# First weights loaded ahead of the constants, low parts of w_out made on VectorE, U blocks redistributed over the routing and gate-matrix stages, gate loads written as three separate thirds

## The chip, the cores and the metric

The kernel runs on one core of a Trainium2 chip. The metric is the device time of one execution in microseconds; smaller is better. Times given as "span" are from the first to the last instruction of one profiled execution.

## What is computed

One decoder block on x of 512 tokens by 1024 channels, all in fp32:

```python
h  = rmsnorm(x) ; z = h @ w_in + b_in              # 1024 x 5376
conv_out = silu(layernorm(conv31(val * sigmoid(gate)))) @ w_conv_out
attn_out = sliding_window_attention(rope(q), rope(k), v, sinks) @ w_attn_o
x  = x + (sigmoid(g_conv)*conv_out + sigmoid(g_attn)*attn_out) @ w_out
h2 = rmsnorm(x)
q  = h2 @ w_pq ; for 8 heads: top 16 of 128 + 128 sub-key scores -> 16 of 16384 experts, softmax gate
x  = x + sum over the chosen experts of gate * gelu(u_emb[e] . h2) * v_emb[e]
out = rmsnorm(x)
```

The tokens form four chunks of 128. For chunk 0 the experts' rows are gathered one by one. For the three other chunks ("dense") the products with all 16384 experts are computed as matrix products: a gate matrix G (experts by tokens, mostly zero) is built, U blocks give gelu(u_emb . h2) for 128 experts at a time, and V steps add (G * gelu) times 128 rows of v_emb.

## The kernel before, in words

Every weight is split into a high part that TensorE multiplies fast and a low rest. `load_w` (L120) does it for one block of 128 x 1024: SP issues the load into `wraw` (L122, three buffers), ScalarE (ACT) rounds it into `whi` (L124, four buffers), and `wlo` is made in one of two ways. With `by_dma` off, VectorE (DVE) subtracts (L130). With it on, ACT writes minus the high part (L127) and a second transfer, issued by GpSimd (POOL, L128), adds the weights from memory to it. `products` (L133) then runs 8 x (high weight by high and by low activation) and 8 x (low weight by high activation): lines L138, L139, L142.

The stages in order of time are:

- Start: SP issues x, g1, ident (L209 to L212), `pc` (L213) and six small constants (L221 to L226); only then come the first weights. Each chunk is normalized and transposed (L183 to L185); the first two blocks of w_in (a gate and a value block) are multiplied in two half-widths by `halves` (L150), and `by_dma` is switched on behind them (L297).
- w_in blocks, rotary tables, the 31-tap convolution on DVE (L283, L286) and the attention, interleaved.
- w_ao and w_co blocks (L441 to L450), then w_out (L458 to L482): two passes of eight weight blocks, each with 12 products of 512 columns (L466, L467, L471), the second pass's halves behind them; after each pass x2 = x + result (L477), the norm, and transposes into tT.
- Routing: for each of eight heads two w_pq blocks, the scores, and the top-16 search on DVE (L495 to L570), each followed by `up(U_HEAD)`, four U blocks (`u_step`, L659).
- Gate matrix: `build_g` (L587), three chunks of eight groups of 16 tokens. DVE makes the one-hot factors (L608, L611), PE multiplies them (L616), ACT copies them out (L618), and SP writes a group to memory (L619). Eight U blocks are handed out over the 24 groups (L708 to L717), so that `AHEAD` = 40 U blocks are done before the last stage.
- Last stage (L728): for i in 0 to 127 one U block (while there are any left) and one V step (18 products, L687 to L689). V steps read the gates of eight steps from one tile `gl` of two buffers, loaded by three transfers (one for each dense chunk, L671) at i % 8 = `GL_AT` = 4 for the next eight steps; DVE multiplies them by the U results (L676), ACT and DVE split them (L680, L681). Beside that POOL gathers the 256 rows of chunk 0 (L624; DVE L639 and L647), paced so that they end at the share `R_V` = 0.99 of the stage's work.

The order of the instructions on each engine isn't the order of the code: a scheduler with a simulated timeline places them, one queue for each engine, and every engine works through its queue in order.

Of the kernel before, what the change touches and what calls it, by code (L numbers as in the profile page):

```python
# [9 lines left out]
F32 = mybir.dt.float32  # L10
# [7 lines left out]
P = 128  # L18
# [9 lines left out]
HEADS = 8  # L28
# [6 lines left out]
DENSE = tuple(b for b in range(NB) if b not in ROW_CHUNKS)  # L35
BUILT = DENSE
ND = len(DENSE)
NU = ND * P
CAND = 80

AHEAD = 40
U_HEAD = 4
ROWS = 4
GT = 16
GI = 8
R_G = 0.0
R_V = 0.99
UC = 3
N_TAPS = 7
XT = 4  # L50
# [2 lines left out]
LOW = 16  # L53
WARM = 0
WARM2 = 0
GL_AT = 4
WRAW = 3
WHL = 4
GLU1 = 4
# [2 lines left out]
J_VAL, J_GATE, J_Q, J_K, J_V, J_GC, J_GA = 0, 8, 16, 24, 25, 26, 34  # L62
# [16 lines left out]
def body(ctx: ExitStack, tc: tile.TileContext, a, out):  # L79
# [10 lines left out]
    def psum(tag):  # L90
        return ps.tile([P, S], F32, name=tag, tag=tag, bufs=2)
# [21 lines left out]
    def load_g(name):  # L113
        g = keep.tile([P, D], F32, name="g")
        nc.sync.dma_start(g, a[name].to_broadcast([P, D]))
        return g

    by_dma = [False]

    def load_w(src):  # L120
        raw = wp.tile([P, D], F32, name="wraw", bufs=WRAW)
        nc.sync.dma_start(raw, src)  # L122
        hi = wp.tile([P, D], F32R, name="whi", bufs=WHL)
        nc.scalar.activation(hi, raw, AF.Copy)  # L124
        lo = wp.tile([P, D], F32R, name="wlo", bufs=WHL)
        if by_dma[0]:
            nc.scalar.activation(lo, hi.bitcast(F32), AF.Copy, scale=-1.0)  # L127
            nc.gpsimd.dma_start(lo, src, accum_op=OP.add)  # L128
        else:
            nc.vector.tensor_tensor(lo, raw, hi.bitcast(F32), op=OP.subtract)  # L130
        return hi, lo
# [39 lines left out]
    def rmsnorm(dst, src, g):  # L171
        ss = small.tile([P, 1], F32, name="n_ss")
        nc.scalar.activation(dst, src, AF.Square, accum_out=ss)
        r = rstd_of(ss, D, [small.tile([P, 1], F32, name=f"n_{x}") for x in "vtr"])
        nc.vector.scalar_tensor_tensor(dst, src, r, g, op0=OP.mult, op1=OP.mult)

    def transpose_split(dst, cs, src):
        hi, lo = dst
        for q in range(2):
            ks = slice(4 * q, 4 * q + 4)  # L180
            p = psum("tr").rearrange("p (a b) -> p a b", a=4)
            for i in range(4):
                nc.tensor.transpose(p[:, i], src[:, (4 * q + i) * P:(4 * q + i + 1) * P], ident)  # L183
            nc.scalar.activation(hi[:, ks, cs], p, AF.Copy)  # L184
            nc.vector.tensor_tensor(lo[:, ks, cs], p, hi[:, ks, cs].bitcast(F32), op=OP.subtract)  # L185

    def chunk(b):
        return slice(b * P, (b + 1) * P)

    def pair_x(name):  # L190
        return [keep.tile([P, KB, S], F32R, name=name + x, tag="x" + x) for x in "hl"]
# [16 lines left out]
    for b in range(NB):  # L208
        nc.sync.dma_start(xs[:, b], a["x"][chunk(b), :])  # L209
        if b == 0:  # L210
            g1 = load_g("g1")
            nc.sync.dma_start(ident, a["ident"])  # L212
    nc.sync.dma_start(pc, a["pc"])  # L213
    h1 = fr.tile([P, NB, D], F32, name="h1", tag="sgc")
    hT = pair_x("hT")
# [239 lines left out]
    h2 = fr.tile([P, NB, D], F32, name="h2", tag="sgc")  # L455
    g2 = load_g("g2")
    tT = pair_x("tT")
    for b0 in range(0, NB, 2):  # L458
        acc = [psum(t) for t in (("ot", "ot", "sc", "sc") if b0 == 0 else ("sc", "sc", "mm", "mm"))]
        for k in range(KB):  # L460
            hi, lo = load_w(a["w_out"][k])
            for c in range(2):
                for n in range(2):
                    ns = slice(n * 512, (n + 1) * 512)
                    p, cs = acc[2 * c + n], chunk(b0 + c)
                    nc.tensor.matmul(p, mT[0][:, k, cs], hi[:, ns], start=(k == 0), stop=False)  # L466
                    nc.tensor.matmul(p, mT[1][:, k, cs], hi[:, ns], start=False, stop=False)  # L467
            for c in range(2):
                for n in range(2):
                    ns = slice(n * 512, (n + 1) * 512)  # L470
                    nc.tensor.matmul(acc[2 * c + n], mT[0][:, k, chunk(b0 + c)], lo[:, ns], start=False,  # L471
                                     stop=(k == KB - 1))
        for c in range(2):
            b = b0 + c
            for n in range(2):
                ns = slice(n * 512, (n + 1) * 512)
                nc.vector.tensor_tensor(x2[:, b, ns], x2[:, b, ns], acc[2 * c + n], op=OP.add)  # L477
            nc.sync.dma_start(x2d[b], x2[:, b])
            rmsnorm(h2[:, b], x2[:, b], g2)
            if b in h2d:  # L480
                nc.sync.dma_start(h2d[b], h2[:, b])
            transpose_split(tT, chunk(b), h2[:, b])  # L482
    fctx.close()

    rp = ctx.enter_context(tc.tile_pool(name="rp", bufs=1, reuse_waits="tile"))
    eidx = rp.tile([P, len(ROW_CHUNKS), SLOTS], U32, name="eidx")
# [170 lines left out]
    gl = {}  # L657

    def u_step(i):  # L659
        w = load_w(a["put"][i])  # L660
        p = psum("mm")[:, :NU]
        products(p, w, [t[:, :, S - NU:] for t in tT])
        g = tp.tile([P, NU], F32, name="ga", bufs=AHEAD + 1)
        nc.scalar.activation(g, p, AF.Gelu)
        ga[i] = g

    def load_gates(i):
        if i < P:
            gl[i // GI] = vp.tile([P, NU // GT, GI, GT], F32, name="gl", bufs=2)
            for n, b in enumerate(DENSE):  # L670
                nc.sync.dma_start(gl[i // GI][:, n * NG:(n + 1) * NG], gv[b][:, :, i:i + GI, :])  # L671

    def v_operands(i):
# [25 lines left out]
    def up(n):  # L699
        for _ in range(n):  # L700
            i = next(ups, None)
            if i is not None:
                u_step(i)

    for h in range(HEADS):
        head(h)
        up(U_HEAD)
    left, groups = AHEAD - HEADS * U_HEAD, len(BUILT) * (P // GT)  # L708
    done = 0
    for b in BUILT:  # L710
        keys(b)
        for _ in build_g(b):
            done += 1
            while done * (AHEAD - HEADS * U_HEAD) > (AHEAD - HEADS * U_HEAD - left) * groups:
                up(1)
                left -= 1
    up(left)  # L717
    by_dma[0] = False
    gctx.close()
    vp = ctx.enter_context(tc.tile_pool(name="vp", bufs=1, reuse_waits="tile"))  # L720
# [3 lines left out]
    rowgen = by_rows()  # L724
    total, due = 2.0 * P - AHEAD, 0.0
    load_gates(0)
    last = {}
    for i in range(P):  # L728
        up(1)
        if i % GI == GL_AT:  # L730
            load_gates(i - GL_AT + GI)
        if i < P - 2:
            v_steps(i)
        elif i == P - 2:
            for _ in rowgen:
                pass
            for n, b in enumerate(DENSE):
                last[n] = rows.tile([P, D], F32, name="row", bufs=ROWS)
                nc.sync.dma_start(last[n], x2d[b])
            v_steps(i, i + 1)  # L740
        due += (2 if i + AHEAD < P else 1) * 2 * SLOTS * len(ROW_CHUNKS) / (R_V * total)
        while due >= 1:
            due -= 1
            next(rowgen, None)
# [59 lines left out]
```

## Time and profile before

| | |
|---|---|
| median of 3 runs | 1836.05 us (1832.74 to 1837.63) |
| the profiled execution's own time | 1836.21 us |
| its span | 1834.4 us, so 1.8 us lie around it |
| PE busy | 1734.7 us (95%) |
| PE weight loads (PEld) | 1519.7 us (83%) |
| DVE busy | 1346.5 us (73%) |
| ACT busy | 918.5 us (50%) |
| POOL busy | 463.9 us (25%) |
| chain that ended last | PE 85%, DMA 5%, DVE 5%, issue 3%, ACT 1% |

PE is TensorE's products, PEld its weight loads. A line such as "L130 DVE" is an instruction group of line 130 on VectorE. The chain that ended last goes back from the last instruction to what released each step. PE is busy for 95% of the span, so the question for a change is in which stretches PE waits or runs at its lower clock, and whose work ends there.

### The profile page before, as it was taken

The page shows a single profiled execution, that of the slowest core. Times are in us where ns is not written, and L with a number is a line of the kernel's source. Part 1 is how long each engine was busy: PE and PEld are TensorE (multiplying, and loading weights), DVE is VectorE, ACT ScalarE, POOL GpSimd, SP SyncE. Part 2 cuts the span into 40 slices and gives each one's busy share as a digit, 9 for nine tenths or more (in the row PEclk, how much of TensorE's full clock was granted, in tenths as well). Part 3 has the DMA queues.
Part 4 walks back from the last instruction along what each step waited for, and adds up shares of the span by engine and source line. Part 5 has one row for each costly group of instructions (what it writes and reads, how often), then busy time and mean ns, then how long its engine had stood idle before and what let it go on. Part 6 is the DMA issues. An engine that isn't in the chain of part 4 may idle for free.

```text
span 1834.4 us, 25060 instructions
## 1 busy us (share of the span) xinstructions
PE 1734.7 (95%) x8892; PEld 1519.7 (83%) x8892; DVE 1346.5 (73%) x2741; ACT 918.5 (50%) x1297; POOL 463.9 (25%) x388
## 2 busy tenths in 40 slices
PE   6999999998899999977599999999999999999996
PEld 6887767786799999966489999999999999988774
DVE  7899992731478787688687768768768767778775
ACT  6449987646565666566533333333333333333332
POOL 1111100112111111000034344424325424434430
PEclk9999998999999999999899999999999999999998
DMA  8996554799999999643678898888889879888884
GB/s 240 230 219 137 132 115 105 172 251 273 254 228 214 225 217 228 199 178 167 229 270 304 271 331 305 294 301 302 308 275 335 304 276 330 309 288 314 302 289 137
DMA packets 167725, 452.21 MB, mean 247 GB/s; under 512 B 14768, under 2 KB 66480, under 8 KB 164528
## 3 DMA queue, kind: packets, MB, share of 16 engines
q0 software_dynamic: 55296, 201.35, 41.8%
q1 hardware_dynamic: 112304, 249.26, 37.9%
q8 instruction: 70, 1.15, 0.2%
q14 instruction: 55, 0.45, 0.1%
HBM read 417.78 MB, written 29.88 MB: 244 GB/s over the span
## 4 chain that ended last, share of the span: by engine, by line
PE 85%; DMA 5%; DVE 5%; issue 3%; ACT 1%; SPq 0%; POOL 0%; DVEq 0%; POOLq 0%; ACTq 0%
PE mm L138 17%; PE mm L139 17%; PE mm L142 17%; PE sc L616 4%; PE tr L689 3%; PE tr L687 3%; PE tr L688 3%; PE sc L688 3%; PE sc L687 3%; PE sc L689 3%; PE ot L687 3%; PE ot L689 3%; PE ot L688 3%; DMA gl<-gb 2%; DMA wlo<-w_out 1%
## 5 line engine op out<-in xcount | busy, mean ns | idle before, releaser
L124 ACT ACTIVATE whi<-wraw 128x1024 fp32r<-128x1024 f32 x346 | 364.9, 1056 | 374.0 <-PE mm L139 200.1
L139 PE MATMUL mm<-tTl,whi 128*128 128x384 f32 (+2 forms) x1168 | 397.5, 341 | 0.2 <-DVE tTl L185 0.2
L138 PE MATMUL mm<-tTh,whi 128*128 128x384 f32 (+2 forms) x1168 | 396.1, 340 | 1.5 <-DVE x L477 1.4
L130 DVE TENSOR_TENSOR wlo<-wraw,whi 128x1024 fp32r<-128x1024 f32 x218 | 265.9, 1221 | 44.3 <-ACT whi L124 40.1
L624 POOL DMA_INDIRECT row<-pu,eidx x128 | 173.0, 1352 | 433.7 <-DVE row L639 270.0
L624 POOL DMA_INDIRECT row<-pv,eidx x128 | 179.8, 1405 | 271.0 <-DVE acc L647 246.6
L680 ACT ACTIVATE wh<-gl 128x384 fp32r<-128x384 f32 x128 | 67.2, 525 | 350.0 <-PE ot L688 321.3
L142 PE MATMUL mm<-tTh,wlo 128*128 128x384 f32 (+2 forms) x1168 | 235.0, 340 | 0.0
L138 PEld LDWEIGHTS mm<-tTh,whi 128*128 128x128 f32 x1168 | 220.3, 189 | 10.0 <-ACT wlo L127 1.8
L139 PEld LDWEIGHTS mm<-tTl,whi 128*128 128x128 f32 x1168 | 220.3, 189 | 8.4 <-DVE tTl L185 0.4
L142 PEld LDWEIGHTS mm<-tTh,wlo 128*128 128x128 f32 x1168 | 204.3, 188 | 3.8
L286 DVE SCALAR_TENSOR_TENSOR yconv<-uc,pc,yconv 128x512 f32<-128x512 f32 x240 | 168.5, 744 | 0.5
L647 DVE SCALAR_TENSOR_TENSOR acc<-row,gate,acc 128x1024 f32<-128x1024 f32 x128 | 163.9, 1280 | 3.6 <-DMA row<-pv,eidx 2.9
L639 DVE SCALAR_TENSOR_TENSOR row<-row,hrow 128x1024 f32<-128x1024 f32 x128 | 155.0, 1220 | 13.7 <-DMA row<-pu,eidx 13.6
L127 ACT ACTIVATE wlo<-whi 128x1024 fp32r<-128x1024 f32 x128 | 134.9, 1055 | 16.6 <-PE mm L142 12.2
L138 PE MATMUL mm<-hTh,whi 128*128 128x512 f32 (+1 forms) x352 | 137.0, 392 | 3.5 <-ACT hTh L184 2.6
L616 PE MATMUL sc<-xt,yt 128*128 128x128 f32 x768 | 110.3, 296 | 31.1 <-DVE xt L611 28.4
L139 PE MATMUL mm<-hTl,whi 128*128 128x512 f32 (+1 forms) x352 | 135.9, 389 | 0.0
L616 PEld LDWEIGHTS sc<-xt,yt 128*128 128x128 f32 x768 | 99.6, 205 | 41.6 <-issue 22.1
L681 DVE TENSOR_TENSOR wl<-gl,wh 128x384 fp32r<-128x384 f32 x128 | 71.1, 556 | 83.1 <-ACT wh L680 78.4
L676 DVE TENSOR_TENSOR gl<-gl,ga 128x384 f32<-128x384 f32 x128 | 61.8, 553 | 90.7 <-DMA gl<-gb 90.7
L618 ACT ACTIVATE gst<-sc 128x512 f32<-128x512 f32 x96 | 99.3, 1064 | 53.5 <-PE sc L616 45.8
(252 smaller groups left out, 3126.3 us busy)
## 6 DMA issues: line engine op xcount, KB each, us to landing
wraw<-put SPq DMA_DIRECT2D x128, 512.0 KB
wraw<-pv SPq DMA_DIRECT2D x128, 512.0 KB
gb<-gst SPq DMA_DIRECT2D x24, 1024.0 KB
gl<-gb SPq DMA_DIRECT2D x48, 512.0 KB
wraw<-w_in SPq DMA_DIRECT2D x42, 512.0 KB
wlo<-w_in POOLq DMA_DIRECT2D x40, 512.0 KB
wlo<-put POOLq DMA_DIRECT2D x40, 512.0 KB
wraw<-w_out SPq DMA_DIRECT2D x16, 512.0 KB
```

The costliest lines, as they stand in the source:

```text
L124: nc.scalar.activation(hi, raw, AF.Copy)
L130: nc.vector.tensor_tensor(lo, raw, hi.bitcast(F32), op=OP.subtract)
L138: nc.tensor.matmul(p, wh[:, ks], xh[:, k], start=(k == 0), stop=False)
L139: nc.tensor.matmul(p, wh[:, ks], xl[:, k], start=False, stop=False)
L142: pace[0] = nc.tensor.matmul(p, wl[:, ks], xh[:, k], start=False, stop=(k == KB - 1))
L286: nc.vector.scalar_tensor_tensor(y[:, j], uc[:, t:t + S], w, y[:, j], op0=OP.mult, op1=OP.add)
L616: nc.tensor.matmul(p[:, t], yt[:, t1 + t], xt[:, t1 + t].rearrange("p a b -> p (a b)"), start=True, stop=True)
L624: ins = nc.gpsimd.indirect_dma_start(out=r, out_offset=None, in_=table, in_offset=bass.IndirectOffsetOnAxis(ap=eidx[:, ROW_CHUNKS.index(b) ...
L647: nc.vector.scalar_tensor_tensor(acc, r, gate[:, b, s:s + 1], acc, op0=OP.mult, op1=OP.add)
L687: nc.tensor.matmul(p, w[0][:, chunk(n)], v[0][:, ns], start=(i == 0), stop=False)
L688: nc.tensor.matmul(p, w[0][:, chunk(n)], v[1][:, ns], start=False, stop=False)
L689: pace[0] = nc.tensor.matmul(p, w[1][:, chunk(n)], v[0][:, ns], start=False, stop=(i == P - 1))
```

## The change

1. Two blocks of w_in are fetched right behind the four chunks of x, ahead of `pc` and the small constants; `load_w` takes them from the list `fetched`.
2. `by_dma` is off for the w_out stage, so that its 16 low parts are made by DVE (L130) and not by ACT (L127) and a transfer (L128); it is on again for the routing stage.
3. U blocks: 4 for each of the first four heads and 3 for each of the others (28, 32 before); 11 over the groups of the gate matrix (8 before); 3 behind it (none before). `AHEAD` is 42 (40 before), so two fewer are left for the last stage.
4. The gate loads of eight steps are issued one at each of i % 8 = 2, 3 and 4, instead of three at 4.
5. `R_V` is 0.96 instead of 0.99: the rows of chunk 0 are gathered at a higher rate and end earlier.

```diff
-AHEAD = 40
-U_HEAD = 4
+AHEAD = 42
+U_HEADS = (4, 4, 4, 4, 3, 3, 3, 3)
+U_LAST = 3
-R_V = 0.99
+R_V = 0.96
-GL_AT = 4
+GL_AT = 2
...
+    fetched = []
+    def fetch(src):
         raw = wp.tile([P, D], F32, name="wraw", bufs=WRAW)
         nc.sync.dma_start(raw, src)
+        return raw
+    def load_w(src):
+        raw = fetched.pop(0) if fetched else fetch(src)
...
+    fetched += [fetch(a["w_in"][j]) for j in (J_GATE, J_VAL)]
     nc.sync.dma_start(pc, a["pc"])
...
     tT = pair_x("tT")
+    by_dma[0] = False
     for b0 in range(0, NB, 2):
...
     fctx.close()
+    by_dma[0] = True
...
-    def load_gates(i):
+    def load_gates(i, blocks=range(ND)):
         if i < P:
-            gl[i // GI] = vp.tile([P, NU // GT, GI, GT], F32, name="gl", bufs=2)
-            for n, b in enumerate(DENSE):
+            if 0 in blocks:
+                gl[i // GI] = vp.tile([P, NU // GT, GI, GT], F32, name="gl", bufs=2)
+            for n in blocks:
+                b = DENSE[n]
                 nc.sync.dma_start(gl[i // GI][:, n * NG:(n + 1) * NG], gv[b][:, :, i:i + GI, :])
...
         head(h)
-        up(U_HEAD)
+        up(U_HEADS[h])
+    spread, groups, done = AHEAD - U_LAST - sum(U_HEADS), len(BUILT) * (P // GT), 0
     for b in BUILT:
         keys(b)
         for _ in build_g(b):
+            up((done + 1) * spread // groups - done * spread // groups)
             done += 1
...
-    up(left)
+    up(U_LAST)
     by_dma[0] = False
...
         up(1)
-        if i % GI == GL_AT:
-            load_gates(i - GL_AT + GI)
+        if 0 <= i % GI - GL_AT < ND:
+            load_gates(i - i % GI + GI, (i % GI - GL_AT,))
```

What the scheduler makes of it is seen in the queues. Lines of the changed kernel have other numbers: its L125 is the load of L122, L137 the subtraction of L130, L486 the addition of L477, L626 the gate product of L616, L145, L146 and L149 the products of L138, L139 and L142, L699 and L700 those of L687 and L688, L683 the gate load of L671. A row counts instructions of the program; PE's fp32 products of L616 appear twice each in a trace.

First DVE's queue at w_out. Before, nothing stands between the last split of `m` and the first addition of the result:

```order
L450 TENSOR_TENSOR ml<-sgc,mh 128x512
L477 TENSOR_TENSOR x_3560<-x_3560,ot 128x512 x2
L477 TENSOR_TENSOR x_3560<-x_3560,sc 128x512 x2
L162 TENSOR_SCALAR n_v<-n_ss 128x1 x2
L164 RECIPROCAL n_r<-n_t 128x1
```

and now:

```order
L458 TENSOR_TENSOR ml<-sgc,mh 128x512
L137 TENSOR_TENSOR wlo<-wraw,whi 128x1024 x6
L486 TENSOR_TENSOR x_3560<-x_3560,ot 128x512 x2
L486 TENSOR_TENSOR x_3560<-x_3560,sc 128x512 x2
L137 TENSOR_TENSOR wlo<-wraw,whi 128x1024
L169 TENSOR_SCALAR n_v<-n_ss 128x1 x2
L171 RECIPROCAL n_r<-n_t 128x1 x2
```

Sixteen subtractions have joined the queue: five between the merge's last blocks, six here, one behind the additions and four behind the first pass's norms.

Second PE's queue at the end of the gate matrix (`sc<-xt,yt` are its products, `mm<-tT..` those of U blocks, `tr<-..,wh` the first V step). Before:

```order
L139 MATMUL mm<-tTl,whi 128x384
L142 MATMUL mm<-tTh,wlo 128x384 x8
L616 MATMUL sc<-xt,yt 128x128 x320
L687 MATMUL tr<-whi,wh 128x512
L688 MATMUL tr<-wlo,wh 128x512
```

and now:

```order
L146 MATMUL mm<-tTl,whi 128x384
L149 MATMUL mm<-tTh,wlo 128x384 x8
L626 MATMUL sc<-xt,yt 128x128 x280
L699 MATMUL tr<-whi,wh 128x512
L700 MATMUL tr<-wlo,wh 128x512
```

In both all U blocks stand ahead of the long run of gate products, and a V step right behind it; the run has become shorter by 40 products. Ahead of it U blocks and half groups of 8 gate products alternate, 8 half groups before and 13 now.

Third SP's queue in the last stage, where the gate loads (`gl`) stand among the loads of `pv`. Before:

```order
L122 DMA wraw<-pv 128x1024 x8
L671 DMA gl<-gb_80 128x8x128
L671 DMA gl<-gb_81 128x8x128
L671 DMA gl<-gb_82 128x8x128
L122 DMA wraw<-pv 128x1024 x10
L739 DMA row<-x2d_76 128x1024
L739 DMA row<-x2d_77 128x1024
L739 DMA row<-x2d_78 128x1024
L122 DMA wraw<-pv 128x1024 x2
L654 DMA out<-wraw 128x1024 x4
```

and now:

```order
L125 DMA wraw<-pv 128x1024 x8
L683 DMA gl<-gb_80 128x8x128
L683 DMA gl<-gb_81 128x8x128
L683 DMA gl<-gb_82 128x8x128
L125 DMA wraw<-pv 128x1024 x5
L748 DMA row<-x2d_76 128x1024
L748 DMA row<-x2d_77 128x1024
L748 DMA row<-x2d_78 128x1024
L125 DMA wraw<-pv 128x1024 x2
L664 DMA out<-wraw 128x1024
L125 DMA wraw<-pv 128x1024 x5
L664 DMA out<-wraw 128x1024 x3
```

The three gate loads still stand side by side with 12 loads of `pv` behind them in both; the loads of x2 (`row<-x2d`) and the first store of the output have moved ahead by five.

## Rows read from the trace of the kernel before

**Rows 1.** Windows: stretch, length; busy us (instructions) of PE, PEld, DVE, ACT, POOL; clock, DMA, GB/s
```profile
0.00:34.30 34.30, 20.36 (x137) 18.98 (x137) 21.84 (x74) 21.80 (x35) 2.19 (x6) 1.00 0.81 252
34.30:263.00 228.70, 228.66 (x1146) 180.57 (x1146) 215.52 (x391) 168.10 (x319) 30.19 (x35) 1.00 0.75 175
412.00:474.00 62.00, 52.47 (x209) 39.69 (x207) 11.38 (x26) 39.24 (x44) 13.85 (x16) 0.92 1.02 271
...
501.57:677.89 176.32, 176.32 (x961) 164.80 (x961) 140.92 (x735) 107.68 (x126) 31.10 (x36) 1.00 0.95 221
...
734.50:774.70 40.20, 40.20 (x276) 40.16 (x275) 26.45 (x39) 23.49 (x28) 2.27 (x2) 1.00 0.61 196
774.70:905.00 130.30, 98.28 (x667) 87.58 (x666) 113.64 (x190) 86.23 (x84) 3.52 (x3) 0.93 0.46 186
905.00:918.00 13.00, 0.24 (x1) 0.24 (x2) 1.41 (x3) 0.95 (x4) 0.00 (x0) 0.54 0.79 260
...
1635.00:1803.60 168.60, 161.60 (x692) 132.56 (x691) 133.60 (x151) 54.73 (x75) 70.29 (x47) 0.97 0.82 287
1803.60:1820.20 16.60, 10.78 (x36) 8.32 (x35) 6.75 (x12) 5.05 (x7) 0.00 (x0) 0.79 0.34 127
```

**Rows 2.** Waits of PE: line, awaited; us in total, times, longest
```profile
PE sc L616 <- DVE xt L611: 28.4, 34, 2.2
PE tr L687 <- ACT wh L680: 13.7, 1, 13.7
...
PE tr L689 <- DVE wl L681: 7.0, 2, 4.1
PE tr L687 <- ACT whi L124: 5.8, 1, 5.8
PE mm L471 <- DMA wlo<-w_out: 4.0, 2, 2.4
PE sc L471 <- DMA wlo<-w_out: 3.3, 3, 2.4
...
PE ot L471 <- DMA wlo<-w_out: 2.2, 4, 0.8
```

**Rows 3.** Chain that ended last, whole span: start, length, what
```profile
3.08 7.18 DMA xs<-x
10.28 5.13 DMA wraw<-w_in
...
432.26 12.65 DMA wlo<-w_out
...
501.57 1.39 PE mm L142 x8
505.73 1.39 PE mm L142 x8
...
1665.62 12.08 DMA gl<-gb
```

**Rows 4.** Waits of DVE, 8 to 40 us
```profile
DVE uc L304 <- ACT sg L300: 2.8, 1, 2.8
```

**Rows 5.** Chain that ended last, in the w_out stage
```profile
412.16 0.24 PE ot L466
...
414.95 0.23 PE ot L466
...
447.03 0.43 PE mm L466
...
454.80 0.87 PE tr L183 x8
...
473.10 0.51 PE sc L471
```

**Rows 6.** Costliest groups: the subtraction; busy, mean ns, idle before
```profile
L130 DVE TENSOR_TENSOR wlo<-wraw,whi 128x1024 fp32r<-128x1024 f32 x218 | 265.9, 1221 | 44.3 <-ACT whi L124 40.1
```

**Rows 7.** Waits of DVE, 1635 to 1810 us
```profile
DVE gl L676 <- DMA gl<-gb: 19.2, 3, 9.4
```

More of the change, by code (lines that the diff above doesn't have):

```diff
@@ L118, in body @@
     by_dma = [False]
-    def load_w(src):
+    fetched = []
+    def fetch(src):
         raw = wp.tile([P, D], F32, name="wraw", bufs=WRAW)
         nc.sync.dma_start(raw, src)
+        return raw
+    def load_w(src):
+        raw = fetched.pop(0) if fetched else fetch(src)
         hi = wp.tile([P, D], F32R, name="whi", bufs=WHL)
@@ L706, in body @@
         head(h)
-        up(U_HEAD)
-    left, groups = AHEAD - HEADS * U_HEAD, len(BUILT) * (P // GT)
-    done = 0
+        up(U_HEADS[h])
+    spread, groups, done = AHEAD - U_LAST - sum(U_HEADS), len(BUILT) * (P // GT), 0
     for b in BUILT:
@@ L712, in body @@
         for _ in build_g(b):
+            up((done + 1) * spread // groups - done * spread // groups)
             done += 1
-            while done * (AHEAD - HEADS * U_HEAD) > (AHEAD - HEADS * U_HEAD - left) * groups:
-                up(1)
-                left -= 1
-    up(left)
+    up(U_LAST)
     by_dma[0] = False
```

## Prediction

> **What bounds the kernel now.** I read the chain of waits for the whole span first: PE carries 85% of it, so a term counts only where PE waits, runs at its lower clock, or has work taken from it. The windows by stage tell where that is [rows 1]. PE is full from 34.3 to 263 (228.66 of 228.70 us), in the six routing heads from 501.57 (176.32 of 176.32, 29.4 for one) and where U blocks and gate products mix (40.20 of 40.20): there only removed work helps. It has holes in the start (20.36 of 34.30), in w_out (52.47 of 62.00, clock 0.92), in the rest of the gate matrix (98.28 of 130.30, clock 0.93), ahead of the first V step (0.24 of 13.00) and at the end (10.78 of 16.60, clock 0.79). PE's waits name the releasers [rows 2]: DVE's one-hot factors for the gate products (28.4 us in 34 waits), the split of the first V step's weights (13.7), the low parts of w_out that arrive by transfer (4.0 + 3.3 + 2.2), and, in the last stage, `wl` (7.0 in two waits) and `whi` (5.8).
>
> **The sum** goes against the profiled execution: 1836.21 us, span 1834.4 with 1.8 around it; the median of the runs, 1836.05, is the same for this purpose. I call 0.3%, 5.5 us, what a measurement can tell from no change.
>
> *First weights.* Before the first product the chain has x landing at 10.28 and then 5.13 us of a w_in load [rows 3], which stands behind `pc` and six small constants on SP. Nothing else is added: two issues trade places with seven on SP, one line later each. Upper bound 5.13, if the weights land with x. Lower bound 0, because chunk 3 still has to be normalized and transposed and DVE follows PE's products. The row between is DVE's idle time of 2.8 us on the first sigmoid [rows 4], which depends on those weights; nothing else that DVE waits for in that stretch goes with them. A loss would need the constants to come too late; they are small, and their first readers come behind the first products. I take **3**, and as PE is full from 34.3 to 263, it is carried through.
>
> *w_out.* A weight block is twelve products; one row starts at 412.16, the next block's at 414.95, so 2.79 us at full clock [rows 5]. Sixteen make 44.6; the two runs of transposes between (0.87 each) make 46.4. The stage runs from 412.16 to 473.61 = 61.4. The difference, 15.1, is what can go: 9.5 us of waits on the transfers [rows 2], and the rest is products that take 0.43 and not 0.23 us behind them (the lower of PE's two levels, 1.2 and 2.4 GHz) [rows 5]. One such transfer takes 12.65 us on the chain [rows 3], in a stretch where the DMA engines are full (1.02) [rows 1]. Now 16 subtractions of 1.22 [rows 6] go to DVE, 19.5 us where DVE has 11.4 of 62 busy [rows 1]: 31 of a stage of 46, so DVE does not become the bound. What queues behind them: the additions of the result (the order shows six subtractions directly ahead). Each waits only for its own load and for the high part that ACT made, and these come before PE's use anyway; but twelve weights would be ahead of the first addition, and there are four `whi`, so one or two subtractions wait until PE has freed a buffer and the additions with them. The second pass writes other banks meanwhile. ACT loses 16 roundings and the DMA engines 16 transfers. Upper bound 15.1. Lower bound: where raw loads set the rate. The stretch moves 271 GB/s [rows 1]; a block of 0.52 MB needs 1.9 us at that rate and 16 of them 31, below the 46, so loads alone cannot hold it; but if each block needed as long as its load and the split one after another, as on the chain now, about half of the gain would stay: 8. I take **14**, near the upper end, as the row that says so is nearest: what stalls there is the transfer that goes. One us is held back because the first routing weights, still by transfer, come behind w_out in a shorter time.
>
> *U blocks.* One takes PE 4.16 us (501.57 to 505.73) [rows 3]. Three fewer in the heads and two fewer in the last stage: 5 x 4.16 = 20.8 off, as PE is full in the heads, and as a U block in the last stage is PE work that fills. Five more stand in the gate matrix, 3 of them written behind it, though the order puts all of them ahead of its long run of gate products. A pair of a half group of gate products and a U block costs 40.20 / 7 = 5.74 [rows 1]. A half group alone is 16 product records, and the long run has 667 in 130.30 us, so 3.13 [rows 1]. The extra U block costs 5.74 - 3.13 = 2.61 rather than 4.16, and five cost 13.1. Net 20.8 - 13.1 = 7.7. Less 1.2, for the DMA engines: U weights still come by two transfers, and share 0.61 in the pairs and 0.95 in the heads [rows 1]. I take **6.5**. Bounds: 20.8, if gate products hide U blocks for nothing; 0, if each moved block costs its full 4.16. A loss needs a wait that is not there now (rival three). The 13.00 us hole ahead of the first V step stays in the sum: no U block stands in it, in the old order or the new.
>
> The Trainium skill ("Perfetto Trace Analysis", Optimization Strategy) says that where the most contended engine changes over time, interleaving those regimes may help. The trace bears this out for seven pairs, where PE is full and DVE has 26.45 of 40.20 [rows 1], yet not at a price of nothing: by the rule taken to its end this term would be 20.8 and the time about 1798.
>
> *Gate loads.* Written at three steps, they stand side by side in SP's queue all the same, with as many `pv` loads before and behind. DVE waits on them three times in the last part, 19.2 us with 9.4 the longest [rows 7], one load takes 12.08 [rows 3], and PE's waits on `wl`, 7.0 [rows 2], come behind. I take **0**; bounds: about 10 off if it did spread them (7.0 and some products at the lower clock: the window has 0.97 [rows 1]), 6 on, if later rows meet one more load.
>
> *Row rate.* Rows of chunk 0 that end earlier take DVE time from the V steps ahead, while the last stretch gets freer. At the end PE waits 5.8 for `whi` [rows 2] behind loads of `pv` that stand behind x2 on SP; five of these loads now stand behind the first store too, which waits for chunk 0's finish. So I expect a similar wait some steps earlier. I take **0**; bounds 6 off (that wait goes and the 0.79 clock of the last 16.60 us [rows 1] rises a bit) and 6 on (a second one of its size).
>
> Sum: 3 + 14 + 6.5 = 23.5, and 1836.2 - 23.5 = **1812.7, say 1812.5**.
>
> **Rivals.**
>
> 1. *w_out gains half.* The loads and the split on DVE hold PE in the second pass: the additions stand behind six subtractions, and the first routing weights come late. For it: DMA at 1.02 [rows 1] though a part of that goes. Against: the waits name the transfer. Gain 8 at most, with a smaller start or U term 1820 or a little over. Chance 0.2.
>
> 2. *Gate products hide the moved U blocks.* DVE bounds the gate matrix (28.4 us of PE's waits [rows 2]), so five more U blocks could fall into them. Against: PE is full in the pairs, and the blocks stand there and not in the long run. 20.8 in place of 6.5: 1798. Chance 0.06.
>
> 3. *Slower.* DVE works in order, and the multiplication by the gates (L676) stands among the row work. With rows denser by 0.99 / 0.96, in the V-only steps DVE runs closer to PE; gate loads of 12.08 us [rows 3] come while the rows' transfers share the DMA engines at 0.82 [rows 1], with the lead of about a dozen `pv` loads only. If a group of gates is late by the present 6.4 us on average (19.2 / 3 [rows 7]), PE loses 3.5 of it (7.0 in two waits [rows 2]) and as much again at the lower clock. Three groups are late now; there are five or so among the V-only steps and eleven ahead of them, whose cover of U work is two blocks less. It takes more than three further late groups to eat the 23.5 of the sum (7 each), and half of the w_out gain gone besides to need only two. Four more, 28 on, give 1840. Against: nothing moves the loads later. Chance 0.03.
>
> 4. *The thirds do take effect.* The text issues them at steps 2, 3 and 4; if they spread, the waits of 7.0 go with the slow products behind: 10 off, 1802.5. The Trainium skill ("Perfetto Trace Analysis", DMA Optimizations) says that splitting DMAs may allow some to start sooner, above all where the DMA engines are mostly idle; the row's share is 0.82, and the order shows no spread, so the trace speaks against it here. Chance 0.06. The split not doing what the text says is my forecast for this part.
>
> 5. *The row rate or the end costs its bound,* 6 on, with a lost start gain, 3: 1821.5. Chance 0.1.
>
> **How the numbers follow.** My forecast has the rest, 0.55: 1807 to 1818, from 5 either way by the bounds of start, U blocks and end. Rivals 1 and 5 reach 1824; on the other side 1802 takes in rival 4. The range **1802 to 1824** leaves out rivals 2 and 3 and the corners where two cases meet, under 0.2. Faster by over 5.5 us (below 1830.5) holds for every case except rival 3 and the far end of 1 and 5 together: 0.94. Within: 0.03. Slower: 0.03.
>
> **What would show it.** In the profile after: PE's first product some 3 us earlier. The w_out stage about 47 us long, no wait on `wlo` from w_out, the clock there at 1.00. Four heads of about 29.4 us and the others of about 25.2. Thirteen pairs at 5.74 us, and the rest of the gate matrix at some 3.13 a half group, five fewer. The 13 us hole unchanged. DVE's waits on `gl` still some 19 us, and PE's on `wl` too. The wait of 5.8 for `whi` moved some steps forward. I am wrong if w_out is longer than 50 us (rival 1), a pair costs less than 5 or more than 6.5 us, the gate waits vanish or multiply, or the last stage is no longer than before less two U blocks by more than 6 us either way.

## The result, and the profile after

The changed kernel takes **1813.95 us** (median of 4 runs, 1812.02 to 1815.70) against 1834.39 before (4 runs): a ratio of 0.9887, with a 95% interval of 0.9867 to 0.9907, so 1.1% or some 20.7 us faster. The forecast was 1812.5. Its profiled execution has a span of 1812.5 us, 21.9 less than the one before.

Where the time went is read by stage, between marks that both programs have: the first and last start of a kind of product (of w_out, of the gate matrix, of the V steps).

| us | before | after | difference | forecast |
|---|---|---|---|---|
| up to the first product of w_out | 412.0 | 409.6 | -2.4 | -3 |
| w_out | 61.9 | 46.1 | -15.8 | -14 (with what follows it) |
| norms and heads, to the first gate product | 260.5 | 246.5 | -14.0 | -12.5 (3 U blocks) |
| gate matrix | 169.4 | 185.6 | +16.2 | +13.1 |
| hole ahead of the first V step | 14.0 | 13.9 | -0.1 | 0 |
| V steps | 904.7 | 899.1 | -5.6 | -8.3 (2 U blocks) |
| after the last product | 11.9 | 11.7 | -0.2 | 0 |

The forecast also set 1.2 us against the gain for shared DMA engines. The windows of the changed kernel's profile (stretch, length; busy us of PE, PEld, DVE, ACT, POOL; PE's clock, DMA share, GB/s), to be laid beside those of [rows 1]:

```profile
409.60:431.90 22.30, 22.30 (x98) 18.08 (x97) 12.13 (x12) 8.71 (x9) 0.00 (x0) 1.00 0.51 168
431.90:456.10 24.20, 24.20 (x113) 19.51 (x111) 14.72 (x29) 17.29 (x23) 2.59 (x3) 1.00 0.80 259
...
702.20:775.81 73.61, 73.61 (x502) 73.57 (x502) 43.77 (x67) 48.43 (x57) 6.22 (x7) 1.00 0.77 230
776.90:887.90 111.00, 83.91 (x552) 74.96 (x550) 95.96 (x161) 72.20 (x69) 3.42 (x3) 0.91 0.46 184
...
887.90:901.70 13.80, 0.19 (x3) 0.03 (x1) 1.20 (x3) 1.63 (x3) 0.00 (x0) 0.59 0.76 253
...
1618.00:1786.60 168.60, 155.22 (x647) 125.92 (x646) 125.79 (x153) 57.10 (x76) 58.04 (x37) 0.95 0.78 271
1786.60:1801.20 14.60, 14.56 (x65) 11.72 (x63) 4.40 (x8) 2.20 (x4) 0.00 (x0) 1.00 0.01 1
```

Both passes of w_out are now full on PE, at full clock. The mix of U blocks and gate products is still full, and longer: 73.61 us from the first gate product to the start of the long run. The rest of the gate matrix and the hole look as they did. In the last stage the stretch ahead of the end is emptier than before (155.22 of 168.60 us, 161.60 before), and the end itself is now full.

PE's waits (line, awaited; us in total, times, longest) beside [rows 2]:

```profile
PE sc L626 <- DVE xt L621: 25.7, 35, 2.2
...
PE tr L701 <- DVE wl L693: 10.5, 3, 3.8
...
PE tr L699 <- ACT whi L131: 2.9, 1, 2.9
```

No wait on a transfer of w_out is left. The wait on `whi` near the end is half of what it was and comes earlier, at 1770.49. The waits on `wl` have grown from 7.0 in two to 10.5 in three. These three became the subject of the experiments.

### The profile page after: what moved, and what is told of

It reads as the page before. It is cut to its first block, busy times and chain, and to the rows that moved or that the text cites. A ratio compares the mean times of both kernels' runs of the same rounds, so it can differ in the third digit from the quotient of the medians.

```text
span 1812.5 us, 25036 instructions
## 1 busy us (share of the span) xinstructions
PE 1726.6 (95%) x8892; PEld 1514.8 (84%) x8892; DVE 1362.7 (75%) x2755; ACT 907.1 (50%) x1287; POOL 457.4 (25%) x374
## 4 chain that ended last, share of the span: by engine, by line
PE 65%; issue 15%; POOL 7%; DVE 6%; DMA 5%; ACT 2%; SPq 0%; POOLq 0%; DVEq 0%; ACTq 0%
PE mm L146 14%; PE mm L145 14%; PE mm L149 14%; POOL row L634 7%; PE sc L626 4%; DMA row<-pv,eidx 2%; PE tr L700 2%; PE tr L701 2%; PE tr L699 2%; PE sc L699 2%; PE sc L700 2%; DMA gl<-gb 2%; PE ot L699 2%; PE sc L701 2%; PE ot L700 2%
## 5 line engine op out<-in xcount | busy, mean ns | idle before, releaser
L145 PE MATMUL mm<-tTh,whi 128*128 128x384 f32 (+2 forms) x1168 | 395.3, 340 | 1.5 <-ACT wlo L134 1.4
L146 PE MATMUL mm<-tTl,whi 128*128 128x384 f32 (+2 forms) x1168 | 396.5, 340 | 0.2 <-DVE tTl L192 0.2
L137 DVE TENSOR_TENSOR wlo<-wraw,whi 128x1024 fp32r<-128x1024 f32 x232 | 283.1, 1223 | 51.0 <-ACT whi L131 50.1
L149 PE MATMUL mm<-tTh,wlo 128*128 128x384 f32 (+2 forms) x1168 | 234.8, 339 | 0.0
L145 PEld LDWEIGHTS mm<-tTh,whi 128*128 128x128 f32 x1168 | 219.6, 188 | 10.0 <-ACT wlo L134 1.8
L146 PEld LDWEIGHTS mm<-tTl,whi 128*128 128x128 f32 x1168 | 219.5, 188 | 8.3 <-DVE tTl L192 0.4
L149 PEld LDWEIGHTS mm<-tTh,wlo 128*128 128x128 f32 x1168 | 204.0, 188 | 3.8
L657 DVE SCALAR_TENSOR_TENSOR acc<-row,gate,acc 128x1024 f32<-128x1024 f32 x128 | 164.1, 1282 | 13.7 <-DMA row<-pv,eidx 7.3
L688 DVE TENSOR_TENSOR gl<-gl,ga 128x384 f32<-128x384 f32 x128 | 61.8, 554 | 104.4 <-DMA gl<-gb 104.4
L145 PE MATMUL mm<-hTh,whi 128*128 128x512 f32 (+1 forms) x352 | 135.9, 389 | 1.0 <-ACT hTh L191 0.8
L146 PE MATMUL mm<-hTl,whi 128*128 128x512 f32 (+1 forms) x352 | 135.2, 387 | 1.6 <-DVE hTl L192 1.6
L626 PE MATMUL sc<-xt,yt 128*128 128x128 f32 x768 | 110.5, 298 | 27.1 <-DVE xt L621 25.7
L626 PEld LDWEIGHTS sc<-xt,yt 128*128 128x128 f32 x768 | 101.2, 208 | 36.0 <-ACT gst L628 20.6
L134 ACT ACTIVATE wlo<-whi 128x1024 fp32r<-128x1024 f32 x114 | 120.2, 1054 | 9.7 <-PE mm L149 9.0
L699 PE MATMUL tr<-whi,wh 128*128 128x512 f32 x256 | 101.3, 398 | 16.5 <-ACT wh L692 13.6
```

Source lines behind the costliest of these rows:

```text
L145: nc.tensor.matmul(p, wh[:, ks], xh[:, k], start=(k == 0), stop=False)
L146: nc.tensor.matmul(p, wh[:, ks], xl[:, k], start=False, stop=False)
L149: pace[0] = nc.tensor.matmul(p, wl[:, ks], xh[:, k], start=False, stop=(k == KB - 1))
L626: nc.tensor.matmul(p[:, t], yt[:, t1 + t], xt[:, t1 + t].rearrange("p a b -> p (a b)"), start=True, stop=True)
L657: nc.vector.scalar_tensor_tensor(acc, r, gate[:, b, s:s + 1], acc, op0=OP.mult, op1=OP.add)
L699: nc.tensor.matmul(p, w[0][:, chunk(n)], v[0][:, ns], start=(i == 0), stop=False)
```

## The experiments

Each ratio is against runs of the kernel before on the same chip; the number behind it is the difference that the ratio makes of 1836 us, with its interval. The first five isolate or undo parts.

**e1, first weights alone** (the kernel before, with the `fetch` lines of the diff):

> The kernel before with the first two weight blocks fetched behind x, and nothing else. In the whole change PE reaches the first product of w_out 2.4 us earlier (409.6 for 412.0). Theory: that is this edit's work and it is carried through, about 1832.0 against some 1834.4 before. Rival: the 2.4 is given back where DVE or a transfer ends a later stage, 1834.4; and by the upper bound of the prediction it would be 5.1, 1829.3.

Measured: 1835.15 us (12 runs), ratio 0.9994 [0.9982, 1.0006]: 1.1 off, between 3.3 off and 1.1 on. The theory's 2.4 and the rival's 0 both lie inside, so no gain in the time is shown for this part alone. PE's first product, at 17.03 us before, is earlier:

```profile
14.98 0.80 PE L145 MATMUL mm<-hTh,whi 128*128 128x256 f32 x2 [0.60 <-ACT hTh L191]
...
26.97 0.39 PE L146 MATMUL mm<-hTl,whi 128*128 128x256 f32 x1 [0.40 <-DVE hTl L192]
```

```profile
27.76 0.28 PE L139 MATMUL mm<-hTl,whi 128*128 128x256 f32 x1
```

The first two lines are of the changed kernel's timeline (start, length; in brackets the idle time before and what ended it), the third is of the kernel before. Products begin at 14.98, with the activations as what PE waits for and no longer the weights. Over the profiles of this study the first product comes at 15.0 to 15.6 us where the weights are fetched early and at 17.0 to 18.0 where they aren't, 2.5 apart; the first product of w_out comes at 410.5 on average against 411.8, 1.3 apart. So about half of it is kept at w_out. The traces show where the lead goes: the 41st product with weights still starts 2.3 us earlier (23.82 for 26.13), the 51st only 0.8 (26.97 for 27.76, the last two lines). Between them the changed kernel transposes its last chunk, from 24.78 on, and PE waits for the activations made of it. In the mean of the profiles the lead falls from 3.0 at the sixth such product to 0.8 at the 51st. Behind that, the order of products differs between the two kernels, and the lead moves up and down before w_out.

**e2, w_out alone**:

```diff
     tT = pair_x("tT")
+    by_dma[0] = False
...
     fctx.close()
+    by_dma[0] = True
```

> The kernel before with the low parts of w_out on VectorE, and nothing else. Theory: the w_out stage becomes 46 us (62 before), PE waits no longer on a transfer there, and the short wait behind it (the first routing product on the addition, 1.4) goes too: 17.3 off, about 1817.1. Rival: a part of this was had only because the U or weight loads around it moved, 12 to 14 off, 1820 to 1822.

Measured: 1823.29 us, ratio 0.9922 [0.9910, 0.9935]: 14.3 off (11.9 to 16.5), so the theory's 17.3 is out. The stage itself does what was expected, 46.1 us:

```profile
413.40:459.90 46.50, 46.50 (x209) 37.61 (x207) 26.84 (x40) 25.99 (x31) 2.60 (x3) 1.00 0.68 214
```

The total is less than the stage's 15.8 and the 1.5 behind it (the 14.0 of the table's heads less three U blocks). That 1.5 wasn't the wait of the first routing product: PE stands still 1.4 us there in this profile and in the changed kernel too, put down to `wlo` on ACT where before it was put down to the addition. It was the routing products behind it, with records of 0.41 us before and 0.28 after. In this profile the first product came 0.9 us later than before, the gate matrix took 1.9 longer and the V steps 2.8 longer, with four stops on `wl` (10.5 us) and not two, though none of this was edited. Stages far from an edit scatter by 2 or 3 us, and the expectation took one profile too literally.

**e8, low parts on DVE in the second pass only** (`by_dma[0] = b0 == 0` in the loop):

> The kernel before with the low parts on VectorE for the second pass of w_out alone; the first pass keeps its transfers. Before, the first pass takes 25.9 us from 412.0 to the last product of its banks and the second 36, against 22.3 and some transposes at full speed. Theory (each pass loses by its own transfers): the second pass's loss goes, about 12 off and the first's 3.4 stays, 1821 to 1823. Rival (the DMA engines are full because of all sixteen transfers, and the second pass's waits are the first pass's backlog): with eight transfers less the first pass loses nothing either, and the whole 17 come, 1817.

Measured: 1825.92 us, ratio 0.9950 [0.9935, 0.9966]: 9.2 off (6.2 to 11.9); w_out takes 49.9 us, 12.0 less. The rival's 17 is out; the theory's stage came, its "about 12 off" in the time lies just outside the interval. The windows of its two passes:

```profile
410.60:436.00 25.40, 22.95 (x96) 17.43 (x94) 5.74 (x6) 13.25 (x13) 4.35 (x5) 1.00 0.96 253
436.00:460.90 24.90, 24.65 (x114) 19.79 (x113) 15.18 (x29) 17.87 (x23) 2.15 (x3) 1.00 0.77 241
```

The first pass keeps its 25.4 us (26.0 before) and the second is nearly as short as in the changed kernel. The first pass loses by its own transfers, and taking away the eight of the second doesn't help it. The second's loss goes with its own eight; how much of it the first pass's transfers would cause alone was not tried.

**e3, U blocks alone** (the `AHEAD`, `U_HEADS`, `U_LAST` lines of the diff):

> The kernel before with the U blocks redistributed (4,4,4,4,3,3,3,3 in the heads, 11 in and 3 behind the gate matrix, 42 ahead), and nothing else. Theory: heads 12.5 shorter, gate matrix 16.2 longer (five blocks at 3.2 each), last stage two blocks of 4.16 shorter, so 4.6 off: about 1829.8. Rival: the last stage gives only the 5.6 that it gives in the whole change, since two blocks less cover the gate loads: 1.9 off, 1832.5.

Measured: 1830.68 us, ratio 0.9965 [0.9952, 0.9978]: 6.4 off (4.0 to 8.8). Its stages are those of the changed kernel: heads 246.7, gate matrix 186.2, V steps 899.4. The theory's 4.6 lies inside, the rival's 1.9 doesn't. The three parts alone add up to 21.8, the whole change to 20.7, so nothing that these intervals can tell is left for the gate loads and the row rate together.

**e4, row rate put back** (`R_V = 0.99` in the changed kernel):

> The changed kernel with the row rate put back to 0.99. Theory: the 2.7 us that the last stage lacks against two blocks of 4.16 are the price of the denser rows (a third stop of PE behind late gates, 3.6 us, less the shorter wait at the end): with 0.99 PE waits on the low gate parts twice (about 7 us) and on the last weights 5.8 at the end, and the time is about 1811.3 against 1814.0 for the changed kernel. Rival: the shortfall comes from the U blocks, the rate as such saves the end: three stops remain and the wait of 5.8 comes back, 1817.

Measured: 1815.60 us, ratio 0.9879 [0.9865, 0.9894]; the changed kernel has 0.9887. The theory fails by its cause: three stops remained (8.8 us) and not two. The wait at the end came back (5.8), as the rival said, yet the time did not rise by the rival's 3; it is 1.5 lower, and the intervals overlap. The number of stops is not set by the rate alone: profiles with 0.99 have two (before, e1, e8), three (e3, e4) and four (e2).

The **thirds** needed no run. With the three loads issued together at step 4, or at step 0, instead of one each at 2, 3 and 4, the scheduler makes the same queues on all five engines, row for row.

**e5, the held U blocks.** The change writes three U blocks behind the gate matrix, and the scheduler moves them ahead of its long run. Here they are held:

```diff
-                        nc.tensor.matmul(p[:, t], yt[:, t1 + t], xt[:, t1 + t].rearrange("p a b -> p (a b)"),
+                        gmm[0] = nc.tensor.matmul(p[:, t], yt[:, t1 + t], xt[:, t1 + t].rearrange("p a b -> p (a b)"),
...
+            if k == 0 and behind is not None:
+                tc.add_manual_dep(m.ins, behind.ins.name,
+                                  mybir.DependencyInfo(mybir.DependencyClass.NoSync, mybir.DependencyReason.DATA),
+                                  reason="behind")
...
-    up(U_LAST)
+    up(U_LAST, gmm[0])
```

> The changed kernel with the three U blocks that its text puts behind the gate matrix really held there: their first product is ordered behind the last gate product on PE. In the queue four U blocks stand in the hole ahead of the first V step, 10 pairs of gate products and U blocks instead of 13. Theory: three pairs less save 3 x 3.2 = 9.7 in the gate matrix, the hole of 13.9 becomes the 16.6 of four U blocks (2.7 more), and one block less in the last stage saves 4.16: 11.1 off, about 1802.9. Rival: the hole is not idle for the other engines, U weights and the gates' round trip through memory get in each other's way, the first V step is later by some of it: 1808 or more. A second rival: U blocks inside the gate matrix cost nothing, the build gets no shorter, and the time is 1812 or more.

Measured: 1806.90 us, ratio 0.9842 [0.9829, 0.9855]: 29.0 off against 20.7 for the changed kernel. The expectation counted the queue wrongly: it has seven half groups ahead of the long run, not ten, so six pairs less than the changed kernel, four U blocks in the hole, and two U blocks more than the changed kernel, not one less, among the V steps (85 for 83; `AHEAD` alone would leave 86, the scheduler moves some ahead of the first V step). Windows of the gate matrix and the hole:

```profile
703.90:875.00 171.10, 138.67 (x917) 128.19 (x916) 133.06 (x222) 113.39 (x116) 9.77 (x10) 0.92 0.57 199
875.00:891.80 16.80, 16.80 (x100) 16.80 (x99) 5.86 (x10) 7.66 (x10) 0.00 (x0) 1.00 0.82 268
```

The hole, 0.19 of 13.80 busy before this edit, is full, and 2.9 us longer because four blocks (16.6) are more than it holds. The gate matrix is 14.5 shorter for six pairs less, 2.4 a pair. The time lies between the theory and the first rival. The miscount worked both ways: the gate matrix gave 14.5 and not 9.7, and the V steps, from which the theory took one block (4.16), became 2.5 longer (901.6 for 899.1). The first V step isn't held up by anything but the fourth block, since PE is full up to it. The second rival, that U blocks inside the gate matrix cost nothing, is excluded.

**e6, gate loads issued by ACT** (`nc.scalar.dma_start` in `load_gates`), and **e7, with the held U blocks**:

> The changed kernel with the gate loads issued by ACT instead of SP, where they don't stand behind loads of V weights that wait for a free buffer. Theory: PE's stops on late gates (10.5 us in three) and the slow products behind them go, some 10 to 15 off in the last 170 us, 1799 to 1804. Rival: the loads are late because the buffer is freed late and the transfer takes 9 to 12 us; then the waits stay and the time is 1814 within 3, or ACT is held up by the wait for the buffer and it is slower.

> Both of the last two edits. If each works at its own place they add up: with 11 off from the held U blocks and 10 to 15 from the gate loads, 1788 to 1793. If only one works, its own time.

Measured: 1837.14 us for e6, ratio 1.0002 [0.9988, 1.0017], and 1833.67 for e7, 0.9995 [0.9982, 1.0008]: the whole gain is lost. ACT's timeline in e6, at the group with the longest issue (ACTq is its queue):

```profile
1699.15 8.59 ACTq L683 DMA_DIRECT2D gl<-gb  x3
1707.87 0.52 ACT L692 ACTIVATE wh<-gl 128x384 fp32r<-128x384 f32 x1 [9.99 <-issue]
```

Issuing these three gate loads takes the queue 8.59 us (2.75 to 8.59 over the sixteen groups), and ACT's work for the V steps stands behind it: the V steps take 921.0 us for 899.1, and PE's waits on `wlo` from 900 us on are 10.5 us where the changed kernel has 0.7, those on `wh` 20.6 for 13.6. DVE's waits on the loads were as long as in the changed kernel (43.2 us in seven from 1350 us on, 42.8 in seven there). So another issuing queue did not shorten these waits, and the question became whether the loads are late at all.

**e9, the multiplications held back.** DVE's queue in the changed kernel, by its instructions near the group that starts at step 104 (L693 makes `wl` of one step, L688 multiplies gates by U results, L657 is row work):

```
L693 TENSOR_TENSOR wl<-gl,wh 128x384
L688 TENSOR_TENSOR gl<-gl,ga 128x24x16 x6
L137 TENSOR_TENSOR wlo<-wraw,whi 128x1024
L688 TENSOR_TENSOR gl<-gl,ga 128x24x16 x2
L657 SCALAR_TENSOR_TENSOR acc<-row,gate,acc 128x1024
L693 TENSOR_TENSOR wl<-gl,wh 128x384
```

All eight multiplications of a group stand together, the first with six low parts of earlier steps still to come. One such place in the trace of the changed kernel, on DVE and then on PE:

```profile
1695.46 3.84 DVE L688 TENSOR_TENSOR gl<-gl,ga 128x384 f32<-128x384 f32 x8 [7.04 <-DMA gl<-gb]
1699.22 1.22 DVE L137 TENSOR_TENSOR wlo<-wraw,whi 128x1024 fp32r<-128x1024 f32 x1
1700.35 1.28 DVE L657 SCALAR_TENSOR_TENSOR acc<-row,gate,acc 128x1024 f32<-128x1024 f32 x1
1701.55 0.56 DVE L693 TENSOR_TENSOR wl<-gl,wh 128x384 fp32r<-128x384 f32 x1
```

```profile
1702.16 0.73 PE L701 MATMUL tr<-whi,wl 128*128 128x512 f32 x2 [3.78 <-DVE wl L693]
...
1704.39 0.63 PE L699 MATMUL tr<-whi,wh 128*128 128x512 f32 x1
...
1706.60 0.39 PE L699 MATMUL sc<-whi,wh 128*128 128x512 f32 x1
```

DVE waits 7.04 us for the load, then does eight multiplications in a row, 3.84 us, and a subtraction and a row, before it makes the one `wl` for which PE stands still. PE is idle 3.78 us and for some 4 us behind it its products run at the lower of its two levels (0.63 us records where 0.39 is usual). The edit puts the multiplication of step i behind the low part of step i - 3 (`LAG` = 3) in DVE's queue:

```diff
+        m = nc.vector.tensor_tensor(w, w, ga[i].rearrange("p (g t) -> p g t", t=GT), op=OP.mult)
+        if i - LAG in low:
+            tc.add_manual_dep(m.ins, low[i - LAG].ins.name,
+                              mybir.DependencyInfo(mybir.DependencyClass.NoSync, mybir.DependencyReason.DATA),
+                              reason="late")
...
+        low[i] = nc.vector.tensor_tensor(wl3, w, wh3.bitcast(F32), op=OP.subtract)
```

> The changed kernel with one ordering on DVE: the multiplication of a step's gates is placed behind the low gate part of the step three before. In the changed kernel's queue the first multiplication of a group of eight stands 6 to 8 low parts ahead of its own, that is right where the scheduler believed the load to have landed. Theory: the loads are early enough for PE and too late only for that early place; the three stops (10.5 us) and the slow products behind them (clock 0.95 in 168 us, some 8) go, 13 to 18 off, 1796 to 1801. Rival: the loads are late as such (they start only when the buffer is freed and take 9 to 13 us); then the stops move to the step that needs them and the time stays 1814 within 3. Second rival: DVE's row work takes the place of the stops, half of it comes, 1806.

Measured: 1799.31 us (1797.27 to 1799.98), ratio 0.9793 [0.9776, 0.9810]: 38.0 off, against 20.7 for the changed kernel, so this ordering is worth some 17 us, give or take 5; the V steps alone are 17.6 shorter in the profiles (881.5 for 899.1). PE's waits from 1300 us on, all of them, and the last 168 us:

```profile
PE tr L705 <- ACT whi L132: 4.2, 1, 4.2
```

```profile
1618.00:1786.00 168.00, 163.84 (x716) 135.05 (x714) 132.44 (x164) 58.94 (x80) 68.41 (x38) 0.99 0.79 277
```

The changed kernel's window of nearly the same stretch is among those shown with the result (1618.00:1786.60). The stops on `wl` are gone, the clock is 0.99 for 0.95, and PE has 716 records of products where it had 647. DVE no longer waits on a gate load there at all, though SP issues the gate loads between the same loads as before. Over the whole last stage DVE's waits on `gl` fall from 90.7 us in thirteen to 13.8 in one, the one ahead of the first V step. The loads were not late for PE. Both rivals fall.

**e10, e9 with the held U blocks, and e11, three U blocks in every head** (`U_HEADS = (3, 3, 3, 3, 3, 3, 3, 3)`):

> That ordering together with the U blocks held behind the gate matrix (e5, which ran at 1806.9). The two work in different stages, so they add: e9's gain on top of e5, 1790 to 1794. If e5's gain came through the last stage, they overlap and it is 1797 or more.

> The same with three U blocks in each head, so that four more go from the first four heads into the gate matrix. Theory: four heads become 4.16 shorter, 16.6 in all, and each block costs 2.4 to 3.2 beside the gate products, 9.6 to 12.8: 4 to 7 below e10. Rival: the first heads are then held by the top-16 search on DVE (23.5 of a head's 25.2 us) or by transfers, and nothing or less is left: e10 within 2.

Measured: e10 1792.70 us, ratio 0.9768 [0.9750, 0.9786]; e11 **1785.35 us**, ratio 0.9713 [0.9695, 0.9731]. On the same chip the medians step by 6.6 and 7.3. The two edits add, and four more U blocks moved into the gate matrix shorten the heads by 17.2 us in the profiles (246.9 to 229.7) and lengthen the gate matrix by 8.3 (170.0 to 178.3), 2.1 each. In e11 the V steps took 7 us longer than in e10 in the one profile each (893.9 and 886.6), and e10's profiled run was its fastest and e11's its slowest, so the profiles alone do not confirm e11; the medians do. The step of 7.3 lies a little over the theory's 4 to 7. e11 beats both kernels, by 2.9% and, by the ratios, some 1.8%.

**e12, e9 with the row rate put back**:

> e9 (the changed kernel with the gate multiplications held back, 1799.3) with the row rate put back to 0.99. Without the stops on late gates, what the rate does is left alone. Theory: it moves only the end: the wait for the last weights becomes 5.8 again instead of 4.2, with a few slow products behind it, 1 to 4 slower, 1800 to 1803. Rival: rows that are less dense leave DVE more room for the V steps, 1797 or less; a second rival: the rate does nothing that can be told, 1799 within 1.

Measured: 1801.30 us, ratio 0.9801 [0.9787, 0.9814] beside e9's 0.9793. The wait at the end is 5.8 again and the V steps took 885.9 us for 881.5, as the theory says, but the intervals overlap. The ratios make the rate of 0.99 slower by 1.5 us here and faster by 1.5 in e4: no effect of the rate on the time is shown, in either direction.

## Why the prediction was right

**The sum.** 23.5 was forecast, 20.7 measured, and the parts came out of the stages that were named. Means over the profiles of this study that share an edit, in place of one pair, are: start -1.3 (2.5 at the first product), w_out -15.9, heads -12.4, gate matrix +14.6, V steps -6.8. They add up to 21.8. Part of the closeness is luck: by these means the start gave 1.7 less than forecast, the U blocks 1.9 less (4.6 for 6.5) and w_out 1.9 more, so the errors partly cancel.

*First weights, 3 forecast.* The cause was right (PE no longer waits for weights), and the first product comes 2.5 earlier. What was too large is the step from there to "carried through": the lead is down to 0.8 by 27 us, ahead of the full stretch that begins at 34.3. What takes it is what the prediction named for its lower bound, the last chunk that still has to be transposed. By w_out 1.3 is left, and in the time alone (e1) none is shown.

*w_out, 14 forecast.* 15.8 in the pair, a little over the upper bound of 15.1, and 14.3 in the time alone (e2). A block at 2.79 us was the right measure: sixteen blocks and the transposes made 46.4, and 46.1 came. The 1 us held back for the routing weights was not needed in the changed kernel's profile, though four later ones show waits on these weights, of 0.2 to 1.1 us (e4, e6, e9, e12). The wait of 1.4 at the first routing product stayed (e2). Rival 1 (half of it) is out: PE is full in both passes, with DVE at 26.9 of 46.5 us. e8 shows that the first pass's loss was its own, and that the second's goes with the second's transfers.

*U blocks, 6.5 forecast.* Alone, 6.4 was measured (4.0 to 8.8), but that it fits so well is luck: the stages give 4.6. The heads are exact (three blocks of 4.16). Two terms were mis-sized. "Five cost 13.1" came as 14.6 in the mean and 16.2 in the one pair of profiles. The price of a half group in the long run, 3.13, was right: the run takes 125.5 us for 40 half groups before (169.4 less the 43.9 below) and 112.0 for 35 after (185.6 less 73.6), 3.1 and 3.2 each. What was too small is the pair, "40.20 / 7 = 5.74": it was read as a half group and a whole U block. In the trace the half groups of the mix stand 23 products apart, and a U block has 24. The mix of the kernel before, up to its long run, beside the line 702.20:775.81 of the changed kernel:

```profile
734.35:778.23 43.88, 43.88 (x302) 43.84 (x302) 29.53 (x44) 26.10 (x31) 2.27 (x2) 1.00 0.59 192
```

The five whole blocks and five half groups (200 records more, 16 + 24 for each) cost 29.7 us, 5.95 each, and all profiles of either kind agree on it. With that price the five cost 14.1. The other term is the last stage: 8.3 forecast for two blocks, 6.8 in the mean. Its profiles have three stops on `wl` where three of the four with two blocks more have two; more than that isn't shown. The 1.2 held back for the DMA engines covered part of both for another reason. The rule of the Trainium skill ("Perfetto Trace Analysis", Optimization Strategy) on interleaving regimes holds in the measured sense: a U block beside the gate products cost 2.1 to 3.2 us where it costs 4.16 alone, and not nothing. Rival 2 is out.

*Gate loads, 0 forecast.* Right, and more strictly than argued: the program is the same with and without the thirds. So the rule on splitting transfers ("Perfetto Trace Analysis", DMA Optimizations, of the Trainium skill), which rival 4 stood on, was not tried by this change; no run here shows what loads that are really spread would do.

*Row rate, 0 forecast.* Right within what can be told (e4, e12). The wait near the end came earlier, as expected, but went from 5.8 to 2.9. Rival 5, 6 on for the rate or the end, is out.

**The step that was wrong, though it cost the forecast nothing**, is the reading of DVE's 19.2 us of waits on `gl` [rows 7]. Rival 3 and the text on the gate loads took them as loads that come late. The profile names the load as what ended the wait, which is true. But DVE had gone to that wait 6 to 8 steps ahead of need, because the order written by the scheduler put it there, and everything behind in its queue stood still with it. e9 shows this: the same loads from the same queue, and behind the first V step neither DVE nor PE waits for them. Rival 3 asked for more than three further late groups; there is one stop more. The size that the prediction gave this place, "about 10 off", fits the two stops of the kernel before. The changed kernel had three: 10.5 us, and behind each some 4 us of products at the lower clock, which lose 2 by an estimate from the one stop shown; together 16.5. e9 gave some 17.

## What to carry to other kernels

When a profile says that an engine waits for a transfer, look in that engine's queue at how far ahead of its use the waiting instruction stands: an instruction placed too early in an engine's queue stalls all that follows, and holding it back with an ordering dependency gave some 17 us here with the same loads. When work is written "behind" a stage, check in the queue that it is there; here it wasn't, and holding it there filled an idle hole. Before a price is read off a repeating pattern, count what one period holds: here it held 23 of a block's 24 products, and the price came out too small.

## What was not expected of the hardware

Issuing the three gate loads of a group held the issuing queue for 2.75 to 8.59 us on ACT (e6), and on SP one of the issues took 7.04 us at the longest, so issuing isn't free for an engine that has work of its own: the move cost some 21 us by the ratios. How much of that is the issue itself and how much what waits behind it wasn't separated. Stages that no edit touched differ by up to 3 us between executions (the V steps of the four kernels with 85 U blocks behind the first V step: 904.6, 904.7, 904.9 and 907.5), which is more than several of the terms argued here.
